# A row gather with deduplication on Trainium2: even and odd rows paired in the PSUM copies, 8 KB stores issued late, slots dealt to groups of 8 partitions

## Chip, cores and metric

One core of one Trainium2 chip. Times are device microseconds (us) of one execution. A run is called *fast* unless it lies more than 1.5% above the fastest of its kernel (*slow*). The profiled execution has a span about 2 us shorter than its timed figure (87.1 against 89.03 for the kernel before); spans are compared with spans and times with times.

## The reference

```python
batch, seq, dim = 32, 512, 1024          # x: (32, 512, 1024) f32, indices: (32, 128) of 0..511
for b in range(batch):
    result[b] = x[b, indices[b]]         # 128 rows of 4 KB for each batch, 16.8 MB in all
```

About 113 of the 128 indices of a batch differ. The kernel therefore loads each distinct row once and lets TensorE copy it to every place that asks for it.

## The kernel before: the parts that matter

The first five batches are gathered whole and stored. For each of the other 27, DVE and PE prepare (`prep`, four batches at a time) which index comes first (`junk`, `cnt`, `lead`), the slot of each distinct row (`slot`, `pack`), the row number for each slot (`at`) and a 0/1 matrix (`s`) that spreads slots to output rows. Then:

```python
HEAD, RING, FAR = 5, 8, 1024
...
# in prep: slots run through consecutive partitions, and the start moves on by 79 each batch
first = (79 * b) % N
turned = turn[:].rearrange("p t n -> p (t n)")[:, N - first:2 * N - first]
...
groups = [(HEAD, HEAD + 3)] + [(g, min(g + 4, B)) for g in range(HEAD + 3, B, 4)]
...
    u = held[(b - HEAD) % RING]                     # a ring of 8 landing tiles
    gather(u, at[:, b:b + 1], b, bounds_check=S - 1, oob_is_err=False)   # POOL; empty slots load nothing
    ps = pout.tile([N, D], F32, name="ps")          # pout: 2 buffers of two PSUM banks each
    for h in range(2):
        nc.tensor.matmul(ps[:, h * 512:(h + 1) * 512], lhsT=spread[b][:],
                         rhs=u[:, h * 512:(h + 1) * 512], start=True, stop=True)
    nc.vector.tensor_copy(out=blocks[b][:, :512], in_=ps[:, :512])
    nc.scalar.copy(out=blocks[b][:, 512:], in_=ps[:, 512:])
    nc.sync.dma_start(out=of[b * N:(b + 1) * N], in_=blocks[b][:])       # 4 KB a partition
```

Of the kernel before, what the change touches and what calls it, by code (L numbers as in the profile page):

```python
# [6 lines left out]
F32 = mybir.dt.float32  # L7
F16 = mybir.dt.float16
I32 = mybir.dt.int32
# [3 lines left out]
@with_exitstack  # L13
def kernel(ctx, tc, x, indices, out):









    nc = tc.nc
    B, S, D = x.shape
    N = indices.shape[1]
    HEAD, RING, FAR = 5, 8, 1024
    assert S <= FAR
    const = ctx.enter_context(tc.tile_pool(name="const", bufs=1))
    ring = ctx.enter_context(tc.tile_pool(name="ring", bufs=1))  # L30
    rows = ctx.enter_context(tc.tile_pool(name="rows", bufs=1))
    pick = ctx.enter_context(tc.tile_pool(name="pick", bufs=1))
    junkp = ctx.enter_context(tc.tile_pool(name="junk", bufs=4))
    PS = bass.MemoryType.PSUM
    pbc = ctx.enter_context(tc.tile_pool(name="pbc", bufs=2, space=PS))
    psm = ctx.enter_context(tc.tile_pool(name="psm", bufs=2, space=PS))
    pout = ctx.enter_context(tc.tile_pool(name="pout", bufs=2, space=PS))


    idx0 = const.tile([N, 1], indices.dtype, name="idx0")  # L40
    nc.sync.dma_start(out=idx0[:], in_=indices.rearrange("b n -> n b")[:, 0:1])
    v4 = const.tile([N, 32], indices.dtype, name="v4")
    for q in range(4):
        (nc.scalar if q % 2 else nc.sync).dma_start(
            out=v4[32 * q:32 * q + 32, :], in_=indices[:, 32 * q:32 * q + 32])
    v = const.tile([B, N], indices.dtype, name="v")
    nc.scalar.dma_start(out=v[:], in_=indices)


    diff = const.tile([N, N], I32, name="diff")  # L50
    nc.gpsimd.iota(diff[:], pattern=[[1, N]], base=0, channel_multiplier=-1)
    turn = const.tile([N, 2, N], I32, name="turn")
    nc.gpsimd.iota(turn[:], pattern=[[0, 2], [1, N]], base=0, channel_multiplier=0)

    def low(t):
        return t[:].bitcast(I32).rearrange("p (n two) -> p n two", two=2)[:, :, 0]

    words = const.tile([N, B], I32, name="words")
    nc.vector.tensor_copy(out=words[:], in_=low(v4))
    idxT = const.tile([N, B], I32, name="idxT")  # L60
    nc.vector.transpose(out=idxT[:], in_=words[:])
    idxF = const.tile([N, B], F32, name="idxF")
    nc.vector.tensor_copy(out=idxF[:], in_=idxT[:])
    vf = const.tile([B, N], F16, name="vf")
    nc.vector.tensor_copy(out=vf[:], in_=low(v))
    ident = const.tile([N, B], F16, name="ident")
    nc.vector.tensor_scalar(out=ident[:], in0=diff[:, :B], scalar1=0, scalar2=None, op0=ALU.is_equal)  # L67
    above = const.tile([N, N], F16, name="above")
    nc.vector.tensor_scalar(out=above[:], in0=diff[:], scalar1=0, scalar2=None, op0=ALU.is_gt)
    below = const.tile([N, N], F16, name="below")  # L70
    nc.vector.tensor_scalar(out=below[:], in0=diff[:], scalar1=0, scalar2=None, op0=ALU.is_lt)
    near = const.tile([N, B], F16, name="near")
    nc.vector.tensor_scalar(out=near[:], in0=idxF[:], scalar1=float(-FAR), scalar2=None, op0=ALU.add)

    xf = x.flatten_outer_dims()
    of = out.flatten_outer_dims()

    def gather(dst, at, b, **kw):
        nc.gpsimd.indirect_dma_start(  # L79
            out=dst[:], out_offset=None,  # L80
            in_=xf[:], in_offset=bass.IndirectOffsetOnAxis(ap=at, axis=0),
            element_offset=b * S * D, **kw)

    blocks = [rows.tile([N, D], F32, name=f"block{b}") for b in range(B)]
    for b in range(HEAD):
        gather(blocks[b], idx0[:].bitcast(I32)[:, 0:1] if b == 0 else idxT[:, b:b + 1], b)
        nc.sync.dma_start(out=of[b * N:(b + 1) * N], in_=blocks[b][:])

    cnt = const.tile([N, B], F32, name="cnt")
    lead = const.tile([N, B], F32, name="lead")  # L90
    lead16 = const.tile([N, B], F16, name="lead16")
    slot = const.tile([N, B], F32, name="slot")
    atF = const.tile([N, B], F32, name="atF")
    at = const.tile([N, B], I32, name="at")
    spread = {}

    def prep(g0, g1):
        n, w = g1 - g0, slice(g0, g1)
        bc = pbc.tile([N, 4, N], F32, name="bc")
        for b in range(g0, g1):  # L100
            nc.tensor.matmul(bc[:, b - g0], lhsT=ident[:B, b:b + 1].to_broadcast([B, N]),  # L101
                             rhs=vf[:], start=True, stop=True)
        for b in range(g0, g1):
            junk = junkp.tile([N, N], F16, name="junk")
            nc.vector.scalar_tensor_tensor(  # L105
                out=junk[:], in0=bc[:, b - g0], scalar=idxF[:, b:b + 1],
                in1=below[:], op0=ALU.is_equal, op1=ALU.mult, accum_out=cnt[:, b:b + 1])
        nc.vector.tensor_scalar(out=lead16[:, w], in0=cnt[:, w], scalar1=0.0, scalar2=None, op0=ALU.is_equal)  # L108
        nc.vector.tensor_scalar(out=lead[:, w], in0=cnt[:, w], scalar1=0.0, scalar2=None, op0=ALU.is_equal)
        sm = psm.tile([N, 2, 4], F32, name="sm")  # L110
        nc.tensor.matmul(sm[:, 0, :n], lhsT=above[:], rhs=lead16[:, w], start=True, stop=True)  # L111
        nc.vector.tensor_copy(out=slot[:, w], in_=sm[:, 0, :n])  # L112
        for b in range(g0, g1):
            first = (79 * b) % N
            pack = junkp.tile([N, N], F16, name="pack")
            turned = turn[:].rearrange("p t n -> p (t n)")[:, N - first:2 * N - first]
            nc.vector.tensor_scalar(out=pack[:], in0=turned, scalar1=slot[:, b:b + 1],  # L117
                                    scalar2=lead[:, b:b + 1], op0=ALU.is_equal, op1=ALU.mult)
            nc.tensor.matmul(sm[:, 1, b - g0:b - g0 + 1], lhsT=pack[:], rhs=near[:, b:b + 1],  # L119
                             start=True, stop=True)  # L120
        nc.vector.tensor_scalar(out=at[:, w], in0=sm[:, 1, :n], scalar1=float(FAR), scalar2=None, op0=ALU.add)  # L121
        nc.vector.tensor_scalar(out=atF[:, w], in0=sm[:, 1, :n], scalar1=float(FAR), scalar2=None, op0=ALU.add)  # L122
        for b in range(g0, g1):
            s = pick.tile([N, N], F32, name=f"s{b}")
            nc.vector.tensor_scalar(out=s[:], in0=bc[:, b - g0], scalar1=atF[:, b:b + 1],  # L125
                                    scalar2=None, op0=ALU.is_equal)
            spread[b] = s

    held = []
    for k in range(RING):  # L130
        u = ring.tile([N, D], F32, name=f"u{k}")
        if k < 3:
            nc.vector.memset(u[:], 0.0)  # L133
        else:
            nc.scalar.copy(out=u[:], in_=held[0][:])  # L135
        held.append(u)

    groups = [(HEAD, HEAD + 3)] + [(g, min(g + 4, B)) for g in range(HEAD + 3, B, 4)]
    done = 0
    for b in range(HEAD, B):  # L140
        while done < len(groups) and groups[done][0] <= b + 8:
            prep(*groups[done])
            done += 1
        u = held[(b - HEAD) % RING]
        gather(u, at[:, b:b + 1], b, bounds_check=S - 1, oob_is_err=False)
        ps = pout.tile([N, D], F32, name="ps")
        for h in range(2):
            nc.tensor.matmul(ps[:, h * 512:(h + 1) * 512], lhsT=spread[b][:],  # L148
                             rhs=u[:, h * 512:(h + 1) * 512], start=True, stop=True)
        nc.vector.tensor_copy(out=blocks[b][:, :512], in_=ps[:, :512])  # L150
        nc.scalar.copy(out=blocks[b][:, 512:], in_=ps[:, 512:])  # L151
        nc.sync.dma_start(out=of[b * N:(b + 1) * N], in_=blocks[b][:])


# [28 lines left out]
```

## Time and profile before

| | kernel before |
|---|---|
| median time, first batch of runs | 89.13 us (88.88 to 89.35, 4 runs) |
| span of the profiled run, granted clock | 87.1 us, 0.971 |
| moved | 32.12 MB, 419 GB/s between 15 and 83 us |
| busy: PE, DVE, ACT, POOL | 58.0, 47.3, 21.9, 32.3 us |
| copies of a product | DVE 691 ns, then ACT 586 ns, 128 partitions x 512 |

PE is TensorE (matmuls), DVE is VectorE, ACT is ScalarE, POOL is GpSimd (it issues the gathers) and SP is SyncE (it issues stores); PSUM is the memory in which PE leaves its products; by a *bank* of it this text means 512 f32 columns. The granted clock is the share of PE's full clock that the records show. A digit in the rows of 40 slices is a busy share in tenths, and GB/s is what the queues moved in the slice. In a group's row, the busy time and the mean length of one instruction come first, then the idle time just before it and what ended most of that. The lines are in the prediction.

### The profile page before, as it was taken

Reading aid. Unit: us, or ns where it says so; the run is one execution under the profiler, and the core shown is the slowest. Engines: PE = TensorE matmul, PEld = TensorE weight load, DVE = VectorE, ACT = ScalarE, POOL = GpSimd, SP = SyncE. Lnnn points to the kernel's source line nnn. Section 1 sums busy time; section 2 is a strip of 40 time slices with the busy share of each in tenths; the row PEclk is TensorE's granted clock in tenths of the full one; section 3 lists DMA queues with packets and bytes.
Section 4 is the critical chain, followed back from the end, with each engine's and each line's share of the span. In section 5 each row is a group of like instructions: output and inputs, shape, how many; then the busy total and the mean of one; then the engine's idle time right before and its main releaser. Section 6 shows DMA issues by size and latency. Waiting matters only on the chain.

```text
span 87.1 us, 784 instructions
## 1 busy us (share of the span) xinstructions
PE 58.0 (67%) x169; PEld 23.9 (27%) x169; DVE 47.3 (54%) x181; ACT 21.9 (25%) x33; POOL 32.3 (37%) x38
## 2 busy tenths in 40 slices
PE   0043502006999999999999999877978877793000
PEld 0031301003434444433443443222322333230000
DVE  4989994107539979587997357833141133333000
ACT  0997000000022222342322234031222222223000
POOL 3577787740354464618545461663200000000000
PEclk9999999999999999999999999999999999999855
DMA  0178999999999999999999999999999999999960
GB/s 4 27 207 224 322 373 363 416 421 418 418 420 420 416 421 418 420 416 421 418 421 410 416 420 427 406 420 420 418 420 418 420 420 414 421 420 420 414 256 15
DMA packets 9603, 32.12 MB, mean 369 GB/s; under 512 B 1751, under 2 KB 1783, under 8 KB 9600
## 3 DMA queue, kind: packets, MB, share of 16 engines
q1 hardware_dynamic: 4848, 16.80, 47.3%
q0 software_dynamic: 4608, 15.24, 45.5%
q10 hardware_dynamic: 144, 0.05, 0.2%
q8 instruction: 1, 0.02, 0.1%
q14 instruction: 2, 0.02, 0.0%
HBM read 16.84 MB, written 16.78 MB: 386 GB/s over the span
## 4 chain that ended last, share of the span: by engine, by line
DMA 35%; DVE 19%; issue 13%; PE 12%; POOL 7%; another core or an unknown queue 3%; ACT 1%; POOLq 1%; DVEq 0%
DMA u<-in_x_dram,at 35%; PE ps L148 11%; POOL u L79 7%; DVE junk L105 6%; DVE pack L117 4%; DVE u L133 2%; DVE block L150 2%; DVE s L125 2%; ACT block L151 1%; POOLq L79 1%; PE bc L101 1%; DVE slot L112 0%; DVE lead L108 0%; PE sm L119 0%
## 5 line engine op out<-in xcount | busy, mean ns | idle before, releaser
L148 PE MATMUL ps<-u,s 128*128 128x512 f32 x108 | 53.2, 629 | 4.5 <-DMA u<-in_x_dram,at 4.2
L79 POOL DMA_INDIRECT u<-in_x_dram,at x27 | 26.7, 990 | 25.5 <-DVE atF L122 9.1
L150 DVE COPY block<-ps 128x512 f32<-128x512 f32 x27 | 18.6, 691 | 22.9 <-PE ps L148 19.1
L151 ACT COPY block<-ps 128x512 f32<-128x512 f32 x27 | 15.8, 586 | 56.3 <-DVE block L150 54.1
L148 PEld LDWEIGHTS ps<-u,s 128*128 128x128 f32 x108 | 19.0, 196 | 29.4 <-issue 27.2
L105 DVE SCALAR_TENSOR_TENSOR junk<-bc,idxF,below 128x128 f16<-128x128 f32 x27 | 8.8, 345 | 0.9 <-issue 0.5
L117 DVE TENSOR_SCALAR pack<-turn,slot,lead 128x128 f16<-128x128 int32 x27 | 7.6, 358 | 2.9 <-remote 2.8
L101 PE MATMUL bc<-vf,ident 32*128 32x128 f16 x27 | 3.3, 263 | 7.7 <-DVE ident L67 5.0
L125 DVE TENSOR_SCALAR s<-bc,atF 128x128 f32<-128x128 f32 x27 | 7.6, 345 | 0.1
L119 PE MATMUL sm<-near,pack 128*128 128x1 f16 x27 | 3.4, 174 | 5.2 <-DVE pack L117 5.0
L119 PEld LDWEIGHTS <-pack 128*128 128x128 f16 x27 | 2.5, 102 | 11.4 <-DVE pack L117 8.2
L101 PEld LDWEIGHTS <-ident 32*128 32x128 f16 x27 | 2.1, 113 | 9.8 <-DVE ident L67 5.0
L135 ACT COPY u<-u 128x1024 f32<-128x1024 f32 x5 | 4.8, 1041 | 0.0
L79 POOL DMA_INDIRECT block<-in_x_dram,idxT x4 | 3.8, 941 | 1.5 <-issue 0.9
L111 PE MATMUL sm<-lead,above 128*128 128x4 f16 (+1 forms) x7 | 1.2, 170 | 3.7 <-DVE junk L105 2.3
L133 DVE MEMSET u<- 128x1024 f32 x3 | 2.7, 912 | 1.3 <-PEq L167 1.0
L121 DVE TENSOR_SCALAR at<-sm 128x4 int32<-128x4 f32 (+1 forms) x7 | 1.1, 162 | 2.5 <-PE sm L119 2.3
L105 DVE DVE_READ_ACCUMULATOR junk<-bc,idxF,below 128x1 f32 x27 | 2.3, 84 | 0.0
L135 ACT ACT_TABLE_LOAD x1 | 1.3, 1283 | 2.1 <-issue 2.1
L111 PEld LDWEIGHTS <-above 128*128 128x128 f16 x7 | 0.7, 103 | 3.7 <-DVE junk L105 2.6
L112 DVE COPY slot<-sm 128x4 f32<-128x4 f32 (+1 forms) x7 | 1.1, 155 | 1.2 <-issue 1.2
L79 POOL DMA_INDIRECT block<-in_x_dram,idx x1 | 1.1, 1098 | 1.6 <-DMA idx<-in_indices_dram 1.6
(17 smaller groups left out, 5.9 us busy)
## 6 DMA issues: line engine op xcount, KB each, us to landing
out_dram<-block SPq DMA_DIRECT2D x32, 512.0 KB, 8.9
u<-in_x_dram,at POOLq DMA_INDIRECT x27
block<-in_x_dram,idxT POOLq DMA_INDIRECT x4
v<-in_indices_dram ACTq DMA_DIRECT2D x2, 8.0 KB
v<-in_indices_dram SPq DMA_DIRECT2D x2, 8.0 KB, 1.8
v<-in_indices_dram ACTq DMA_DIRECT2D x1, 32.0 KB
idx<-in_indices_dram SPq DMA_DIRECT2D x1, 1.0 KB
block<-in_x_dram,idx POOLq DMA_INDIRECT x1
```

Source lines behind the costliest of these rows:

```text
L79: nc.gpsimd.indirect_dma_start(out=dst[:], out_offset=None, in_=xf[:], in_offset=bass.IndirectOffsetOnAxis(ap=at, axis=0), element_offset= ...
L101: nc.tensor.matmul(bc[:, b - g0], lhsT=ident[:B, b:b + 1].to_broadcast([B, N]), rhs=vf[:], start=True, stop=True)
L105: nc.vector.scalar_tensor_tensor(out=junk[:], in0=bc[:, b - g0], scalar=idxF[:, b:b + 1], in1=below[:], op0=ALU.is_equal, op1=ALU.mult, ac ...
L111: nc.tensor.matmul(sm[:, 0, :n], lhsT=above[:], rhs=lead16[:, w], start=True, stop=True)
L117: nc.vector.tensor_scalar(out=pack[:], in0=turned, scalar1=slot[:, b:b + 1], scalar2=lead[:, b:b + 1], op0=ALU.is_equal, op1=ALU.mult)
L119: nc.tensor.matmul(sm[:, 1, b - g0:b - g0 + 1], lhsT=pack[:], rhs=near[:, b:b + 1], start=True, stop=True)
L125: nc.vector.tensor_scalar(out=s[:], in0=bc[:, b - g0], scalar1=atF[:, b:b + 1], scalar2=None, op0=ALU.is_equal)
L133: nc.vector.memset(u[:], 0.0)
L135: nc.scalar.copy(out=u[:], in_=held[0][:])
L148: nc.tensor.matmul(ps[:, h * 512:(h + 1) * 512], lhsT=spread[b][:], rhs=u[:, h * 512:(h + 1) * 512], start=True, stop=True)
L150: nc.vector.tensor_copy(out=blocks[b][:, :512], in_=ps[:, :512])
L151: nc.scalar.copy(out=blocks[b][:, 512:], in_=ps[:, 512:])
```

## The change

The intent is longer packets: two neighbouring output rows lie side by side in one partition, so that a store writes 8 KB runs. Without moving data between partitions, the selection matrix puts even rows on partitions 0 to 63 and odd rows on 64 to 127, and the PSUM copies put the two halves side by side; two batches fill a tile of 128 partitions. Stores go out two pairs late, to leave the queues to the gathers. Slots are dealt round 16 groups of 8 partitions, so that the empty ones are spread. The start is changed as well: four whole batches, a second early index column, a later `turn` table.

```diff
-    HEAD, RING, FAR = 5, 8, 1024
+    HEAD, RING, FAR, LAG, CUT = 4, 8, 1024, 2, 704
...
+            nc.gpsimd.iota(turn[:], pattern=[[0, 2], [1, 16], [16, N // 16]], base=0, channel_multiplier=0)
...
-            first = (79 * b) % N
+            at0 = (3 * b) % 16 * (N // 16)
...
-            nc.vector.tensor_scalar(out=s[:], in0=bc[:, b - g0], scalar1=atF[:, b:b + 1],
+            nc.vector.tensor_scalar(out=s[:].rearrange("p (two m) -> p two m", two=2),
+                                    in0=bc[:, b - g0].rearrange("p (m two) -> p two m", two=2), scalar1=atF[:, b:b + 1],
...
+    def store(k, after):
+        lo = (HEAD + 2 * k) * N
+        with tc.issue_after(after.ins):
+            nc.scalar.dma_start(
+                out=of[lo:lo + 2 * N].rearrange("(p two) d -> p (two d)", two=2), in_=pairs[k][:])
...
-    groups = [(HEAD, HEAD + 3)] + [(g, min(g + 4, B)) for g in range(HEAD + 3, B, 4)]
+    groups = [(HEAD, HEAD + 2)] + [(g, min(g + 4, B)) for g in range(HEAD + 2, B, 4)]
...
-        nc.vector.tensor_copy(out=blocks[b][:, :512], in_=ps[:, :512])
-        nc.scalar.copy(out=blocks[b][:, 512:], in_=ps[:, 512:])
-        nc.sync.dma_start(out=of[b * N:(b + 1) * N], in_=blocks[b][:])
+        to = pairs[k][half * H:(half + 1) * H, :]          # H = 64
+        nc.scalar.copy(out=to[:, :D], in_=ps[:H, :])
+        nc.vector.tensor_copy(out=to[:, D:D + CUT], in_=ps[H:, :CUT])
+        last = nc.scalar.copy(out=to[:, D + CUT:], in_=ps[H:, CUT:])
+        if half and k >= LAG:
+            store(k - LAG, last)
```

More of the change, by code (lines that the diff above doesn't have):

```diff
@@ L37 @@
     pout = ctx.enter_context(tc.tile_pool(name="pout", bufs=2, space=PS))
-    idx0 = const.tile([N, 1], indices.dtype, name="idx0")
-    nc.sync.dma_start(out=idx0[:], in_=indices.rearrange("b n -> n b")[:, 0:1])
+    first = []
+    for b, eng in ((0, nc.sync), (1, nc.scalar)):
+        t = const.tile([N, 1], indices.dtype, name=f"first{b}")
+        eng.dma_start(out=t[:], in_=indices.rearrange("b n -> n b")[:, b:b + 1])
+        first.append(t[:].bitcast(I32)[:, 0:1])
     v4 = const.tile([N, 32], indices.dtype, name="v4")
@@ L51 @@
     nc.gpsimd.iota(diff[:], pattern=[[1, N]], base=0, channel_multiplier=-1)
-    turn = const.tile([N, 2, N], I32, name="turn")
-    nc.gpsimd.iota(turn[:], pattern=[[0, 2], [1, N]], base=0, channel_multiplier=0)
     def low(t):
@@ L82, in gather @@
             element_offset=b * S * D, **kw)
-    blocks = [rows.tile([N, D], F32, name=f"block{b}") for b in range(B)]
+    blocks = [rows.tile([N, D], F32, name=f"block{b}") for b in range(HEAD)]
+    pairs = [rows.tile([N, 2 * D], F32, name=f"pair{k}") for k in range((B - HEAD) // 2)]
+    turn = const.tile([N, 2, 16, N // 16], I32, name="turn")
     for b in range(HEAD):
-        gather(blocks[b], idx0[:].bitcast(I32)[:, 0:1] if b == 0 else idxT[:, b:b + 1], b)
+        if b == 2:
+            nc.gpsimd.iota(turn[:], pattern=[[0, 2], [1, 16], [16, N // 16]], base=0, channel_multiplier=0)
+        gather(blocks[b], first[b] if b < 2 else idxT[:, b:b + 1], b)
         nc.sync.dma_start(out=of[b * N:(b + 1) * N], in_=blocks[b][:])
@@ L113, in prep @@
         for b in range(g0, g1):
-            first = (79 * b) % N
+            at0 = (3 * b) % 16 * (N // 16)
             pack = junkp.tile([N, N], F16, name="pack")
-            turned = turn[:].rearrange("p t n -> p (t n)")[:, N - first:2 * N - first]
+            turned = turn[:].rearrange("p t e j -> p (t e j)")[:, at0:at0 + N]
             nc.vector.tensor_scalar(out=pack[:], in0=turned, scalar1=slot[:, b:b + 1],
@@ L131 @@
         u = ring.tile([N, D], F32, name=f"u{k}")
-        if k < 3:
+        if k < 2:
             nc.vector.memset(u[:], 0.0)
@@ L149 @@
                              rhs=u[:, h * 512:(h + 1) * 512], start=True, stop=True)
-        nc.vector.tensor_copy(out=blocks[b][:, :512], in_=ps[:, :512])
-        nc.scalar.copy(out=blocks[b][:, 512:], in_=ps[:, 512:])
-        nc.sync.dma_start(out=of[b * N:(b + 1) * N], in_=blocks[b][:])
+        k, half = divmod(b - HEAD, 2)
+        H = N // 2
+        to = pairs[k][half * H:(half + 1) * H, :]
[4 more added lines that the diff above has]
+            store(k - LAG, last)
+    for k in range((B - HEAD) // 2 - LAG, (B - HEAD) // 2):
+        store(k, last)
 _INS = ['x', 'indices']
```

## The prediction

> **What bounds the kernel now.** I read the page's 40 slices first, then the groups, the waits of each engine, a stretch of the timeline, and last the chain of waits.
>
> ```profile
> DMA  0178999999999999999999999999999999999960
> GB/s 4 27 207 224 322 373 363 416 421 418 418 420 420 416 421 418 420 416 421 418 421 410 416 420 427 406 420 420 418 420 418 420 420 414 421 420 420 414 256 15
> DMA packets 9603, 32.12 MB, mean 369 GB/s; under 512 B 1751, under 2 KB 1783, under 8 KB 9600
> ```
> A slice is 87.1/40 = 2.18 us. From the eighth slice (15 us) to the last but two (83 us) the queues move about 419 GB/s without a dent: 32.12 MB / 0.419 = 76.7 us of the 87.1. **The transfers are the bound**; the rest is a start of some 10 us in which they are not yet full.
>
> ```profile
> L148 PE MATMUL ps<-u,s 128*128 128x512 f32 x108 | 53.2, 629 | 4.5 <-DMA u<-in_x_dram,at 4.2
> L150 DVE COPY block<-ps 128x512 f32<-128x512 f32 x27 | 18.6, 691 | 22.9 <-PE ps L148 19.1
> L151 ACT COPY block<-ps 128x512 f32<-128x512 f32 x27 | 15.8, 586 | 56.3 <-DVE block L150 54.1
> ```
> The matmuls take 53.2/27 = 1.97 us a batch, the two copies 0.69 and 0.59. The third row matters most: ACT is idle 56.3 us, 54.1 of it until *DVE's copy of the same product* is done, though the two copy different halves. The timeline (start, length) shows the hand-over:
>
> ```profile
> 58.30 1.96 PE L148 MATMUL ps<-u,s 128*128 128x512 f32 x4 [0.53 <-DMA u<-in_x_dram,at]
> 58.53 0.59 ACT L151 COPY block<-ps 128x512 f32<-128x512 f32 x1 [1.45 <-DVE block L150]
> ...
> 60.29 0.69 DVE L150 COPY block<-ps 128x512 f32<-128x512 f32 x1 [1.79 <-PE ps L148]
> ...
> 61.02 0.59 ACT L151 COPY block<-ps 128x512 f32<-128x512 f32 x1 [1.90 <-DVE block L150]
> ```
> PE ends at 60.26, DVE starts at 60.29 and ends at 60.98, ACT starts at 61.02. So copies of one product run one after the other, 0.03 to 0.04 us apart. It costs nothing now: with two product buffers a buffer's round is 1.96 + 0.69 + 0.59 + 0.1 = 3.3 us, under the two batches (3.9 us) that PE needs, and under the two batches of transfers.
>
> [...] 1040 ns for 1024 columns from SBUF, 586 for 512 from PSUM[...]. [...] a 4096 B packet takes 159 ns, two lone 8192 B instruction fetches 309 ns, not 318. [...] no view of the profile names the engine of a packet.
>
> **The change part by part.**
>
> *8 KB stores.* 14 pair stores x 128 packets = 1792 packets of 309 ns for 3584 of 159: (3584 x 159 - 1792 x 309)/16 = 1.0 us of all engines saved. Batch 4 becomes a deduplicated one: about 15 rows, 0.06 MB, 0.15 us. The second early index load starts the second gather perhaps 0.5 us sooner. Together **about -1.5 us, if the transfers stay the bound.**
>
> *Copies.* One product now has three copies by the built program: ACT the lower 64 partitions, 1024 columns; then DVE the upper ones, 704 columns, which waits for that ACT copy; then ACT the last 320, which waits for DVE; and PE's product after next waits for that last one. [...] ACT's order in the program is lower(b), lower(b+1), rest(b), rest(b+1), then a store.
>
> *The new loop.* Let PE start b at 0. It ends b at 1.96 and b+1 at 3.85. ACT: lower(b) 2.0 to 3.0, **lower(b+1) 3.9 to 4.9**, then rest(b) to 5.3 (DVE's share of b ended at 3.95). Only then may PE start b+2, at 5.4 to 5.5. So a pair takes **5.45 us**, against 2 x (464 + 524) KB = 1.98 MB / 0.42 = 4.7 us of transfers and 3.9 us of matmuls. The bound moves from the transfers to this round: PE stands idle 1.6 us in each pair.
>
> *The preparation on DVE.* DVE's fixed order puts most of a four-batch preparation (4 counts at 0.27, 4 packs in 1.12, 4 selections in 1.1, small ones: some 4 us) between the copies of one pair and those of the next, where the loop leaves it 2.6 us; and part of it waits for PE's small products, which stand behind the big ones in PE's order. Following the order by hand with the durations above, from the first product's start T: the last copy of pair 0 ends at T+7, pair 1 T+13, 2 T+18.6, then 3 T+25.6, 4 T+33, 5 T+40 (7 to 7.5 each: for pair 3, PE ends b+1 at 21.5, slot at 21.8, packs to 23, a count to 23.3, only then DVE's copy to 24.3). From pair 6 nothing is left to prepare: T+45.8, and 7 more pairs x 5.5 give T+84.
>
> *Start.* T: gathers go out 1.25 to 1.3 us apart, and by the packets the first deduplicated one, with four whole gathers ahead of it instead of five, lands near 16 us. DVE and PE stand still now and then between 14 and 19.6 us in the kernel before (DVE 2.84 us by "remote"), which may fall here too. T = 16.3 to 19, say 17.5.
>
> *End.* Last copy near 17.5 + 84 = 101.5. The last three pair stores are issued only after it: 0.4 us for the issue, 1.5 to 2 until data flows, 3.15 MB / 0.425 = 7.4 us, 1.6 us from the last packet to the end as now. Span about 112.5. The timed median was 89.34 where the profile's span was 87.1, so add 2: **114 us.**
>
> **Rivals.**
> 1. *The transfers stay the bound and the packets pay.* 89.3 - 1.5 = 87.8 us, or 86 with a better start. For it: the slices at 419 GB/s. Against it: it needs 4.7 us a pair, and the round of the two product buffers is 5.45 by measured durations and built waits. It would be right only if the ACT copy of 64 partitions were far cheaper than 1.0 us, and nothing shows a copy that depends on partitions.
> 2. *The loop without the preparation's delay.* If DVE's order cost nothing, 14 pairs at 5.5 plus 2: last copy near T+78, end near 106 us. For it: the kernel before hides the same preparation. Against it: there DVE copies as soon as PE is done, here it stands in line behind an ACT copy.
> 3. *Late stores leave the queues empty, and uneven dealing.* [...] Here the queues have slack, so it shows little. The empty stretch before the first pair store (some T+18.6) costs nothing either when copies are the bound, but the three stores at the end are fully exposed: some 10 us, in my sum already.
>
> **Range and chances.** The loop and its 13 repeats carry the figure: 0.1 us wrong in a pair is 1.4 us. Start is good for 3 us, the preparation for 6. So 114, 107 to 120. Faster only if rival 1 holds: 0.03. Within 2%: 0.03, a half-hidden version of it. Slower: 0.94.
>
> **What would show it.** Right: ACT's largest wait is for DVE's copy or for PE, PE idles 1.5 us or more in each pair until an ACT copy, products of the last pairs start 5.4 to 5.6 us apart by twos, GB/s falls to 350 or so with holes between 25 and 35 us, and 3 MB of stores follow the last copy. Copies of 1.01, 0.89 and 0.43 us; packets of 8192 B near 309 ns. Wrong: GB/s at 420 up to the end, copies of one product at the same time, or an ACT copy well under 1 us. Preparation mis-sized: pairs 3 to 5 at 5.5 instead of 7.

What no trace or run of this case shows is cut from the prediction and from three expectations below, and the cuts are marked. What is left of the paragraph before *The change part by part* was read from the trace of the kernel before: 1040 and 586 ns are ACT copies, 318 is twice 159. The sum came to a span of 112.5 us (17.5 to the first product, 84 to the last copy, 11 to the end), and with the 2 us between span and time to 114. The costs of the three copies came to 1.01, 0.89 and 0.43 us and enter the 5.45 us of a pair: they rested on costs per column that no trace had shown. The 1.5 to 2 us until data flows are my estimate; from issue to landing an 8 KB index load took 1.8 us in the kernel before.

## The result, and the profile after

The changed kernel takes 115.3 us (114.36 to 115.64, 4 fast runs), against 89.13 us of the kernel before: ratio 1.292, 95% interval 1.2825 to 1.3016. Ratios here are the mean time of one kernel's fast runs over that of the other's in the same rounds, so not quite the ratio of the medians. The profiled run's span is 112.6 us at a granted clock of 0.941.

The page of the changed kernel, 40 slices of 2.8 us:

```profile
PEclk9999999999999999599999999999999999997555
DMA  1399999988966799957878889999998918263993
GB/s 10 71 322 309 349 386 413 405 274 268 332 185 201 211 384 291 381 172 221 343 239 301 300 236 408 298 413 339 413 329 341 381 49 329 93 279 140 419 419 140
```

The even row of 420 GB/s is gone; from the ninth slice on the queues pass 400 GB/s only in single slices, and stay there for two only at the very end, when the last stores are alone. The same page's groups, with L165 the product and L170, L171, L172 the three copies:

```profile
L165 PE MATMUL ps<-u,s 128*128 128x512 f32 x112 | 57.0, 652 | 22.7 <-ACT pair L172 18.3
L170 ACT COPY pair<-ps 64x1024 f32<-64x1024 f32 x28 | 28.1, 1005 | 40.3 <-PE ps L165 21.6
...
L171 DVE COPY pair<-ps 64x704 f32<-64x704 f32 x28 | 25.0, 894 | 29.9 <-ACT pair L170 29.6
...
L172 ACT COPY pair<-ps 64x320 f32<-64x320 f32 x28 | 11.8, 422 | 12.8 <-DVE pair L171 12.6
```

Each stage's idle time names the one ahead of it, in a ring: PE waits for L172, L172 for L171, L171 for L170, L170 for PE. No transfer stands among these releasers. One turn of the ring, from the timeline late in the run (start, length, in brackets the idle time before and its releaser):

```profile
85.66 0.42 ACT L172 COPY pair<-ps 64x320 f32<-64x320 f32 x1
...
86.14 3.70 PE L165 MATMUL ps<-u,s 128*128 128x512 f32 x8 [1.54 <-ACT pair L172]
...
88.16 1.01 ACT L170 COPY pair<-ps 64x1024 f32<-64x1024 f32 x1 [1.14 <-PE ps L165]
...
89.19 0.89 DVE L171 COPY pair<-ps 64x704 f32<-64x704 f32 x1 [2.63 <-ACT pair L170]
...
89.87 1.00 ACT L170 COPY pair<-ps 64x1024 f32<-64x1024 f32 x1 [0.71 <-PE ps L165]
...
90.90 0.42 ACT L172 COPY pair<-ps 64x320 f32<-64x320 f32 x1
...
91.38 3.70 PE L165 MATMUL ps<-u,s 128*128 128x512 f32 x8 [1.54 <-ACT pair L172]
```

The two products of a pair start at 86.14, the next two at 91.38: 5.24 us a pair, with PE idle for 1.54 of them. The copy that frees the first buffer (90.90) stands in ACT's queue behind the 1.00 us copy of the *second* product. This period of 5.24 us repeats without change over the last eight pairs.

The end, by the windows of both kernels (columns: stretch and its length, then the busy time of PE, PEld, DVE, ACT, POOL, the granted clock, the DMA share, GB/s), here the changed kernel's:

```profile
102.00:112.60 10.60, 0.00 (x0) 0.00 (x0) 0.29 (x1) 0.42 (x1) 0.00 (x0) 0.54 0.72 297
```

The last copy ends at 102.7, and the remaining 9.9 us are three stores of 1 MB with nothing beside them.

### The profile page after: what moved, and what is told of

It is laid out like the page before. It is cut to its first block, busy times and chain, and to the rows that moved or that the text cites. A ratio compares the mean times of both kernels' runs of the same rounds, so it can differ in the third digit from the quotient of the medians.

```text
span 112.6 us, 812 instructions
## 1 busy us (share of the span) xinstructions
PE 63.5 (56%) x176; PEld 26.5 (24%) x176; DVE 56.3 (50%) x190; ACT 47.0 (42%) x63; POOL 32.8 (29%) x38
## 4 chain that ended last, share of the span: by engine, by line
PE 51%; ACT 15%; DVE 13%; DMA 9%; issue 2%; ACTq 1%; DVEq 0%; POOLq 0%
PE ps L165 49%; ACT pair L170 10%; DMA u<-in_x_dram,at 7%; ACT pair L172 5%; DVE pair L171 4%; DVE pack L127 3%; DVE junk L115 2%; DMA v<-in_indices_dram 2%; DVE slot L122 1%; PE sm L129 1%; DVE lead L118 1%; PE sm L121 0%; DVE ident L72 0%; ACTq L51 0%; ACTq L47 0%
## 5 line engine op out<-in xcount | busy, mean ns | idle before, releaser
L165 PE MATMUL ps<-u,s 128*128 128x512 f32 x112 | 57.0, 652 | 22.7 <-ACT pair L172 18.3
L170 ACT COPY pair<-ps 64x1024 f32<-64x1024 f32 x28 | 28.1, 1005 | 40.3 <-PE ps L165 21.6
L84 POOL DMA_INDIRECT u<-in_x_dram,at x28 | 27.8, 994 | 44.7 <-PE ps L165 25.0
L171 DVE COPY pair<-ps 64x704 f32<-64x704 f32 x28 | 25.0, 894 | 29.9 <-ACT pair L170 29.6
L165 PEld LDWEIGHTS ps<-u,s 128*128 128x128 f32 x112 | 21.1, 203 | 50.4 <-ACT pair L172 25.6
L172 ACT COPY pair<-ps 64x320 f32<-64x320 f32 x28 | 11.8, 422 | 12.8 <-DVE pair L171 12.6
L152 ACT COPY u<-u 128x1024 f32<-128x1024 f32 x6 | 5.8, 1041 | 0.0
L84 POOL DMA_INDIRECT block<-in_x_dram,first x2 | 2.0, 1020 | 2.0 <-DMA first<-in_indices_dram 1.7
L150 DVE MEMSET u<- 128x1024 f32 x2 | 1.8, 912 | 1.2 <-PEq L191 1.0
L84 POOL DMA_INDIRECT block<-in_x_dram,idxT x2 | 1.9, 944 | 0.5 <-issue 0.5
```

The costliest lines, as they stand in the source:

```text
L84: nc.gpsimd.indirect_dma_start(out=dst[:], out_offset=None, in_=xf[:], in_offset=bass.IndirectOffsetOnAxis(ap=at, axis=0), element_offset= ...
L152: nc.scalar.copy(out=u[:], in_=held[0][:])
L170: nc.scalar.copy(out=to[:, :D], in_=ps[:H, :])
L171: nc.vector.tensor_copy(out=to[:, D:D + CUT], in_=ps[H:, :CUT])
L172: last = nc.scalar.copy(out=to[:, D + CUT:], in_=ps[H:, CUT:])
```

## The experiments

My theory: the round of the two product buffers through PE, ACT, DVE, ACT bounds the kernel. The rivals: late stores (empty queues before, exposed stores after), uneven dealing, the packets themselves. Medians below are of all runs of a kernel, slow ones too; ratios are of fast runs alone.

**1. Two copies in place of three**

```diff
-        nc.vector.tensor_copy(out=to[:, D:D + CUT], in_=ps[H:, :CUT])
-        last = nc.scalar.copy(out=to[:, D + CUT:], in_=ps[H:, CUT:])
+        last = nc.vector.tensor_copy(out=to[:, D:], in_=ps[H:, :])
```

> The changed kernel with two copies a product (ACT the lower half, DVE the whole upper half, 1024 columns) in place of three. Theory of the round: DVE's copy becomes 0.16 + 1.07 = 1.22 us, the last ACT copy of 0.42 us and its wait behind the next product's lower copy go; PE may start b+2 at 4.4 us instead of 5.24, so a pair takes 4.45 us and the 8 to 10 pairs that have no preparation in their way save 0.8 us each: 105 us, 101 to 108, with 28 copies of 1.22 us on DVE. Rival (late stores and uneven dealing are the cost): the copies do not matter, 115 us stays.

Measured: 105.11 us median; only one of the four runs counts as fast, with 102.74 us, so there is no ratio with an interval. That one is still 11.6 us below the fastest run of the changed kernel. The profiled run (slow, 104.83 us) shows the new period, from 87.46 to 91.81, 4.35 us for a pair, where 4.45 was expected (the 1.22 us for DVE's copy was an estimate; the line through the traces' 691 ns for 512 columns and 894 for 704 gives 1.23, and 1.227 was measured):

```profile
87.46 3.70 PE L165 MATMUL ps<-u,s 128*128 128x512 f32 x8 [0.68 <-DVE pair L171]
...
90.53 1.23 DVE L171 COPY pair<-ps 64x1024 f32<-64x1024 f32 x1 [1.45 <-ACT pair L170]
...
91.81 3.70 PE L165 MATMUL ps<-u,s 128*128 128x512 f32 x8 [0.65 <-DVE pair L171]
```

DVE now does more work than before (1.23 us a product for 0.89), and the kernel is faster: what counted was the length of the chain, not the load of DVE. ACT's load did fall, but in the changed kernel's loop (60 to 102 us) ACT was busy for only 22.8 of 42 us.

**2. No waits between the copying engines**

```diff
-        ps = pout.tile([N, D], F32, name="ps")
+        pa = pout.tile([N, 512], F32, name="pa")      # one bank each
+        pb = pout.tile([N, 512], F32, name="pb")
...
+        nc.vector.tensor_copy(out=to[:, :512], in_=pa[:H, :])
+        nc.vector.tensor_copy(out=to[:, D:D + 512], in_=pa[H:, :])
+        nc.scalar.copy(out=to[:, 512:D], in_=pb[:H, :])
+        last = nc.scalar.copy(out=to[:, D + 512:], in_=pb[H:, :])
```

> The changed kernel, but each product in two one-bank tiles: DVE copies both partition halves of the first 512 columns, ACT those of the other 512, so that no copy waits for another engine's. Pairs, 8 KB stores, late stores and dealing stay. Theory of the round: it falls to 1.96 + 2 x 0.69 = 3.4 us a buffer, PE (3.9 us a pair) or the transfers (4.7) are the bound again; most of the loss is given back: 94 us, 91 to 98, the rest of it being the three exposed stores at the end. Rival late stores: 105 or more, because the queues stay empty until the first pair store and after the last copy. Rival uneven dealing: 99 or more.

Measured: 97.68 us (96.73 to 98.27; two of the four runs are slow), ratio to the kernel before 1.093 (1.0835 to 1.1033). The bytes copied are the same, the pairs, the late stores, the dealing and the packets stay, and 17.6 of the 26.2 us are given back. This decides between the theory and the rivals: the chain between engines was most of the loss. What is left has a new bound, by the window of the middle of this run (fast):

```profile
35.00:60.00 25.00, 21.64 (x63) 8.28 (x61) 24.25 (x77) 11.59 (x21) 8.81 (x10) 1.00 1.01 397
```

DVE, the third figure in the list, is busy 24.25 of 25 us. It now makes two copies of 0.68 us a product where the kernel before made one of 0.69 (64 of 128 partitions cost the same time for half the data), and POOL waits 25.0 us in this run for the row numbers that DVE prepares.

**3. No lag, in the changed kernel**

```diff
-    HEAD, RING, FAR, LAG, CUT = 4, 8, 1024, 2, 704
+    HEAD, RING, FAR, LAG, CUT = 4, 8, 1024, 0, 704
```

> The changed kernel with each pair stored as soon as it is copied (lag of 0 instead of 2 pairs). Theory of the round: the loop is the same, only the end is shorter, one store of 1.05 MB instead of three after the last copy, 2.1 MB / 0.42 = 5 us less: 110.3 us, 109 to 112. Rival (late stores are the main cost): below 100 us.

Measured: 111.83 us, ratio 1.246 where the change has 1.292, that is about 4 us (0.046 x 89.5). Confirmed in direction and nearly in size. In the profile (slow) the end after the last copy shrinks from 9.9 to 5.3 us, and pairs 1 and 2 take 7.2 and 8.4 us instead of 5.9 and 5.1, so in this run a part of the gain at the end is lost earlier. DVE makes both copies of a pair only after the packs there, and the clock is at half in two stretches of the loop instead of one (the 58 and the 85 in the page's PEclk row; PE is busy for 64.9 us, in the changed kernel for 63.5). No fast run of it was profiled, so this is not shown for the fast ones.

**4 and 5. The dealing, in the kernel before**

```diff
-            first = (79 * b) % N
+            at0 = (3 * b) % 16 * (N // 16)      # run 4: turn = iota [[0,2],[1,16],[16,8]], as in the change
+            first = 4 * ((3 * b) % 32)          # run 5: turn = iota [[64,2],[1,8],[16,4]], base 8h, for each half h
```

> The kernel before with the dealing to groups of 8 partitions alone. [...] up to 5 us more, 91 to 94.5 us. If [...] the queues even it out: 88.5 to 89.7 us, unchanged. The theory of the round says nothing of it.

> The kernel before, its slots dealt so that each set of partitions 4i to 4i+3 and those 32 further on gets its share (one empty place in each of the 16 sets). [...] this one must not lose: 88.3 to 89.6 us, with the last 10 us of transfers at 419 GB/s instead of 320. If any dealing that breaks up a run of partitions is bad: 91 to 93.

Both expectations rested on my assumption of which partitions share a DMA engine; the 5 us of the first and the layout of the second came from it.

Measured: the change's dealing alone makes the kernel before slower, 92.93 us, ratio 1.0335; the dealing by sets does not, 89.22 us, ratio 0.999 (0.9908 to 1.0071). The GB/s rows of both pages, first the change's dealing (that profile is of a slow run, 93.1 us, but fast runs show the ratio), then the dealing by sets:

```profile
GB/s 5 25 225 237 293 372 376 419 417 417 419 417 413 419 415 413 413 422 415 419 417 419 417 412 417 419 419 413 424 419 419 415 386 320 329 322 325 325 119 7
```

```profile
GB/s 4 27 204 240 283 369 386 420 420 418 422 416 416 401 407 416 405 386 409 416 420 401 411 420 418 420 420 418 420 418 420 418 418 418 420 420 420 420 308 8
```

With the first dealing nothing is to be seen up to the 32nd slice, then the queues fall to 320 to 329 GB/s, for 11 us; with the second they hold 418 to 420 to the 38th. The mean busy share of the 16 DMA engines falls with the rate, from nine tenths or more to seven or eight (the page's DMA row). That fits engines that have run out of work while others are behind, but it is not shown. Both dealings break up the runs of partitions, and only the first costs anything, so a broken run is not in itself what costs; what in the first does is not shown.

**6. The dealing undone, in the changed kernel** (the four lines of the kernel before for `turn` and `first`)

> The changed kernel with the dealing of the kernel before. Theory of the round: the copies set the pace and the queues have slack, so what costs 3.4 us in the kernel before costs nothing here: 114.3 to 116, unchanged. If costs simply add: 112.

Measured: 113.17 us (112.87 to 113.55), ratio 1.262. A miss: I expected no change. The two profiled runs have the same clock (0.940 and 0.941), and the undealt one's span is 1.0 us shorter, 111.6 for 112.6; its last copy of pair 0 ends at 26.8 instead of 27.8, and every later pair keeps that lead. Of this lead 0.6 us is there when the first product starts (17.98 instead of 18.58), after the one stretch in which transfers are the bound here too (416 GB/s from 16 to 18.6 us in the changed kernel). The rest goes with the clock: the clock records begin, at full clock, 1.1 us after the second product's start in the undealt run and 1.8 us after it in the other, and that product takes 2.52 us instead of 2.86. The other microsecond between the medians goes with the clock: three of the changed kernel's four timed runs were granted 0.91, all of these 0.94. How often the clock drops was not under my control.

**7 to 9. What is left of the one-bank kernel: lag, dealing, packets, one after the other**

```diff
-    HEAD, RING, FAR, LAG, CUT = 4, 8, 1024, 2, 704      # 7, on top of experiment 2
+    HEAD, RING, FAR, LAG, CUT = 4, 8, 1024, 0, 704
-            at0 = (3 * b) % 16 * (N // 16)              # 8, on top of 7
+            at0 = N - (79 * b) % N                      # with the consecutive turn table
-                out=of[lo:lo + 2 * N].rearrange("(p two) d -> p (two d)", two=2), in_=pairs[k][:])   # 9, on top of 8
+                out=of[lo:lo + 2 * N].rearrange("(p two) d -> p two d", two=2)[:, j, :],   # j = 0, 1
+                in_=pairs[k][:, j * D:(j + 1) * D])
```

> The kernel of the run with one-bank products, with each pair stored as soon as it is copied. Late stores as a cost of their own: after the last copy one store instead of three (2.1 MB, 5 us), and the queues filled between 25 and 35 us: 93 us, 91.5 to 95.5. If the stores' lateness is hidden there: 97 to 98, unchanged. It should stay above the kernel before by the uneven dealing (3.4 us when done alone) less the 8 KB packets' 1 us.

> The same with the dealing of the kernel before (the empty slots in one run of partitions, moved on by 79 each batch). Uneven engines: transfers end 3 us sooner, 90 us, 88.5 to 92. If DVE, whose copies of 64 partitions take twice as many instructions, sets the pace by now: 92.5 to 95, little gained.

> The kernel of the run with one-bank products, early stores and the old dealing, each pair stored by two DMAs of 4 KB rows instead of one of 8 KB. The packets alone: 1792 x 2 x 159 - 1792 x 309 ns over 16 engines is 1.0 us more, if the transfers are the bound there, plus 14 issues of 0.35 us on ACT, which has room: 0.5 to 1.5 us slower than that run. If something else bounds it: within 0.5 us of it.

Measured: 96.93 us (ratio 1.085, 1.0772 to 1.092), 97.04 (1.074, 1.0636 to 1.0841) and 93.53 (1.047, 1.0327 to 1.0604). The first is a miss: with DVE as the bound, early stores gave no gain that is clear of the noise (1.093 before them, and the intervals overlap). The second missed both of its ranges; only "little gained" came true, and this step too is within the noise. The third is a miss with the wrong sign: **two stores of 4 KB packets are faster than one of 8 KB** by 2.7% of the kernel before, although the same records give 309 ns for an 8192 B packet and 159 for a 4096 B one. The time from issue to landing of a deduplicated gather (the last figure), first with 8 KB stores (this profile is of a slow run, 98.07 us), then with 4 KB (fast):

```profile
u<-in_x_dram,at POOLq DMA_INDIRECT x28, 10.1
```

```profile
u<-in_x_dram,at POOLq DMA_INDIRECT x28, 8.5
```

A gather's median goes from 10.1 to 8.5 us. That the longer packets of the stores hold up the gathers is my guess. The landing times of these two agree with it, but they don't depend on the packets alone: with 4 KB stores in experiment 5 the median is 11.5 us. The edit also splits each store into two DMAs, and the first of them goes out before the pair is wholly copied (at 75.59 us, when the pair's last copy starts; with 8 KB the issue follows the last copy). No run separates the length of the packet from the split, so the packet stays a possible cause, not a shown one.

**10 and 11. DVE's second copy given to ACT, stores issued by SP**

```diff
-        nc.vector.tensor_copy(out=to[:, D:D + 512], in_=pa[H:, :])
+        last = nc.scalar.copy(out=to[:, D:D + 512], in_=pa[H:, :])
-            nc.scalar.dma_start(
+        nc.sync.dma_start(
```

> The kernel of one-bank products, early stores and old dealing, with DVE's second copy of a product given to ACT and the stores issued by SP. There DVE was busy 24 us of 25 and held up the indices of later gathers. If DVE was the bound: DVE's 69 us of work fall by 19, 92 us, 90 to 94.5. If the 8 KB stores[...] were what made it slow: 95 to 97.

> The same with two DMAs of 4 KB rows for each pair. If 8 KB packets hurt only by taking bandwidth from the gathers while DVE is late: within 1 us of the run with 8 KB, 90 to 93. If they hurt by themselves: 3 us faster than that run. A pure gain of bandwidth from 8 KB would make this one 1 us slower.

Measured: 92.86 us with 8 KB stores (ratio 1.035, 1.0248 to 1.0449), 91.41 with 4 KB (1.0205, 1.014 to 1.0271). The edit moves a copy and the stores at once, and drops the fixed place of the store after the last copy; no run separates these. That DVE's load held the one-bank kernel fits: DVE's busy time falls from 68.7 to 49.8 us between the profiles with 8 KB (the first of a slow run), and the ratio from 1.074 to 1.035. Even so, 8 KB stores lose 1.45 us by the medians to 4 KB ones; every fast run with 8 KB is slower than every run with 4 KB, though the intervals overlap. I had expected at most 1 us if DVE's lateness were the reason. Between 35 and 80 us both (fast) profiles move the same, 413 to 417 and 417 to 418 GB/s. They part at the end: between 84 and 86 us the 8 KB kernel falls to 82 GB/s, its last pair being copied until 85.3, while the other, whose copies end at 82.0, moves 336. So in neither of the two pairs of kernels did the longer packet pay.

**12. The start alone, in the kernel before** (`HEAD` 4, the second early index column, the later turn table, first groups of 2 and 4)

> The kernel before with the changed start alone: four whole gathers instead of five, the second index column loaded by itself, the turn table written after two gathers. The second gather can go out about 0.5 us sooner and 0.06 MB less is read; the transfers are the bound from 15 us on, so at most 0.15 + 0.5 us: 88.6 us, 88.0 to 89.5.

Measured: 90.88 us, ratio 1.0147 (1.0084 to 1.0209). A miss with the wrong sign. The windows of 25 to 30 us, first the kernel before, then this one:

```profile
25.00:30.00 5.00, 5.00 (x20) 2.22 (x19) 3.91 (x19) 1.76 (x3) 2.58 (x3) 1.00 1.03 417
```

```profile
25.00:30.00 5.00, 5.00 (x21) 2.02 (x20) 3.50 (x14) 1.26 (x3) 3.78 (x5) 1.00 0.88 245
```

The queues fall from 417 to 245 GB/s: 5 us x 172 GB/s = 0.86 MB, or 2.1 us at 417. The likely reason stands in POOL's timeline, the last gather before a pause and the first after it, of the kernel before and then of this one:

```profile
17.40 0.99 POOL L79 DMA_INDIRECT u<-in_x_dram,at  x1 [0.30 <-issue]
23.08 0.99 POOL L79 DMA_INDIRECT u<-in_x_dram,at  x1 [4.70 <-DVE atF L122]
```

```profile
16.97 0.99 POOL L80 DMA_INDIRECT u<-in_x_dram,at  x1 [0.30 <-issue]
22.92 0.99 POOL L80 DMA_INDIRECT u<-in_x_dram,at  x1 [4.96 <-DVE atF L126]
```

Both pause for 5 us until DVE has the next row numbers. Before the pause, the kernel before has issued 5 + 7 gathers, this one 4 + 6, as its first groups prepare 2 + 4 batches and not 3 + 4. The backlog of two gathers fewer, some 0.9 MB, no longer covers the pause. The size fits the loss; no run changes the first groups alone, so this is argued and not shown.

**The account.** Each run as a ratio to the kernel before:

| step | ratio |
|---|---|
| the change | 1.292 |
| its copies on one-bank tiles | 1.093 |
| + stores at once | 1.085 |
| + the old dealing | 1.074 |
| + one copy from DVE to ACT, stores by SP (8 KB) | 1.035 |
| + 4 KB stores | 1.0205 |
| the start of the change alone, on the kernel before | 1.0147 |

If the costs add, the last two rows leave some half a per cent for the paired copies themselves, once no engine waits for another; their intervals overlap, so it may be nothing. No version beat the kernel before; the one dealt by sets (experiment 5) cannot be told from it. What I did not try, for want of runs: the last kernel of the ladder with the old start.

## Why the prediction was right

The predicted time was 114, the measured 115.3, and the span 112.6 where 112.5 had been worked out. The agreement of the total is better than that of its terms, and so far it is luck. All are read from the changed kernel's timeline:

| term | predicted | measured |
|---|---|---|
| copies | 1.01, 0.89, 0.43 us | 1.005, 0.894, 0.422 us |
| packet of 8192 B | 309 ns | 309 ns (median of 1792) |
| first product T | 17.5 us | 18.58 us |
| pair 0, after T | 7 | 9.2 |
| pairs 3, 4, 5, each | 7, 7.4, 7 | 6.67, 8.48, 6.88 |
| a pair of the plain loop | 5.45 to 5.5 | 5.24 |
| last copy | 101.5 | 102.7 |
| from there to the end | 11 | 9.9 |

- **The bound.** Right as the prediction put it: the round of the buffers, with PE idle until an ACT copy (25.6 us by the weight loads' waits). Experiment 1 shortened the chain and moved the period from 5.24 to 4.35; experiment 2 removed the chain and most of the loss.
- **The preparation.** Right in mechanism: pairs 3 to 5 are the long ones, and by the timeline DVE's copies start after the packs. Rival 2, a preparation hidden as before, is refuted by these three pairs. (Its T+78 is T+79 by its own sum, 14 x 5.5 + 2. DVE's copies took 691 ns for 512 columns, 894 for 704 and, in experiment 1, 1227 for 1024, that is 1.04 to 1.06 ns for each further column.)
- **Terms that were mis-sized.** The start was 2.2 us too short in pair 0. Its first product takes 4.1 us, not 2: the first two half products last 2.07 us each where later ones take 1.0. The first clock record of this run, of full clock, begins at 24.3 us (where nothing is recorded the views show 1.00), so a half clock before it is likely by the lengths alone and not recorded. One stretch at 0.5 is recorded inside the loop, 3.4 us from 44.8 us, the 5 in the PEclk row. From 41.5 us PE had had nothing but the preparation's small products, 1.1 us of work in three, and the two products that followed took 5.40 us instead of 3.70. So pair 4's excess of 1.7 us over its neighbours goes with that half clock, which itself came after a wait. The loop was taken 0.2 us too long for each pair, 1.5 us over the last seven, and the tail 1.1; these errors cancel the first ones.
- **The rivals.** Rival 1, that packets pay under an unchanged bound, fell twice: the bound moved, and where the transfers were the bound again for most of the time (experiments 10 and 11) the longer packets did not pay. The prediction's term of -1 us for 8 KB stores did not come true there, nor in experiments 8 and 9, where DVE was the bound; it did no harm only because it was not in the sum. Rival 3 was right about the end (9.9 us exposed, 4 us of it saved by no lag) and about a dealing that costs little here (0.6 us); that it costs several us under a transfer bound, experiment 4 measured (3.4 by medians, 3.0 by the ratio).
- **The better start** was given as worth up to 0.5 us. The second gather does go out 0.45 us sooner (4.18 for 4.63), but the start alone costs 1.5%: the step that failed counted when the first gathers go out, not how many are on the way when the row numbers are late.

## What to carry to other kernels

Before splitting a PSUM copy, read who waits for whom among the copies you have: if two engines already take turns on one product, a third copy lengthens the buffer's round, and with two buffers the round, not any engine's load, became the period here (5.24 us a pair with three copies, 4.35 with two). A copy of 64 partitions cost as much time as one of 128 (0.68 to 0.69 us on DVE and 0.58 to 0.59 on ACT, both for 512 columns), so pairing rows this way doubles the copying. Measure a longer packet in the kernel, not by its own duration: one of 8192 B took 309 ns and two of 4096 B 318, yet a pair stored by one DMA of 8 KB packets gave 97.0 us against 93.5 with two of 4 KB packets, and 92.9 against 91.4; how much of that is the packet and how much the split is open.

## What else the records show

- **Waits between copies.** In these builds copies of different column halves (before, ACT idle 54.1 us behind DVE) and of different partition halves (after, DVE idle 29.6 us behind ACT) waited for each other as long as they shared a tile. With a tile of its own for each half of the columns (experiment 2) no copy's wait names a copy on another engine (the view of its waits), and the median fell from 115.3 to 97.7 us.
- **ACT copies.** From SBUF, the memory the gathers land in, 1024 columns took 1040 ns; from PSUM 1005 ns for 1024 columns and 422 for 320 on 64 partitions, that is 0.83 ns a column and 157 ns beside; on 128 partitions 586 ns for 512.
- **The clock.** One stretch of 3.4 us at half clock inside a loop bound by waits cost 1.7 us (5.40 for 3.70). The window before it was not idle: PE was busy for 1.28 of its 3.41 us. The traces of the kernels before and after, cut from their first clock record on at steps of that length (busy as the profile models it), have three windows at full clock with 1.28 us or less of matmuls (0.38, 0.92 and 1.28), each followed by half clock; all others have 1.87 us or more, four of the changed kernel's loop just that, and each was followed by full clock. What lies between is not shown.
